# Experts of middle rank as 64- and 32-place float32 units instead of three-pass float32r, in one layer of a hybrid network on Trainium2

## The chip, the cores and the metric

One core of one Trainium2 chip. The metric is device time in microseconds (us) of one execution. The kernel before was timed three times: 1410.18, 1393.49 and 1408.15 us, median 1408.15.

## What is computed

One layer: RMSNorm, an input projection, four parallel sequence branches, an output projection with residual, then a mixture of experts with its own RMSNorm, router and residual, and a final RMSNorm. There are 512 tokens of width 1024, all float32. The change touches the mixture of experts alone:

```python
logits = xt @ router_w + router_b
top_logits, top_idx = lax.top_k(logits, 4)
gates = softmax(top_logits)
# for each of 32 experts e, for the tokens that chose it:
hmid = xt[tok] @ w_gu[e] + b_gu[e]                # 1024 -> 2048
glu  = minimum(hmid[:, 0::2], 7.0)
lin  = clip(hmid[:, 1::2], -7.0, 7.0)
act  = glu * sigmoid(1.702 * glu) * (lin + 1.0)
y    = act @ w_down[e] + b_down[e]                # 1024 -> 1024
out[tok] += gate * y
```

Each expert has 8 MB of `w_gu` and 4 MB of `w_down`, so 384 MB of weights pass through the core once.

## The kernel before

The first 350 us compute the branches and the router. Then `moe` (L495) runs the 32 experts one after the other in an order written as a string, `SEQ` (L56). The experts are ranked on the chip by how many tokens chose them; a rank has a fixed number of places (`HCAP`, `LCAP`, L53), and tokens beyond it go to an extra loop that runs only if there are any.

An expert is one or two *units* (class `Unit`, L513):

- **H** (heavy; ranks 0 to 12, up to 128 places): the tokens' activations stand still in TensorE, the weights stream past as float32r. For the precision of float32 weights and activations are each split in a high and a low part, and three products are made: high by high, high by low, low by high (`three`, L640). Weights are split by `Splits.make` (L619): ScalarE writes the high part (L627), VectorE the low part (L628), for 1024 columns at a time, into one of `NSP` = 3 buffers `w2`. A heavy expert needs 24 such splits.
- **L** (light; 64 places): plain float32 matmuls straight from the weights (L672, L741). The 2048 hidden columns are two output halves that stand on partitions 0 to 63 and 64 to 127, so two matmuls run side by side.
- **B** (32 places): the same with four matmuls side by side. Only rank 0 has one, for its places 129 to 160, beside its H unit; this pair is called the big expert below.

The loop at L866 works on expert j: the first product `gemm1` over eight 1 MB weight chunks k (L887), the activation function `act` (L677), then the second product `gemm2` of expert j-1 over eight halves f of its down chunks (L930), so that the activation of j is hidden behind it. `back` (L693) transposes the activated values of j for its own `gemm2`. `yout` (L746) multiplies by the gate and makes high and low parts of the result on ScalarE and VectorE; for a unit of 32 places that is four instructions on each, for one of 64 two. `hot` makes a 0/1 matrix S of places and tokens, and `add` (L784) scatters the results of all pending units with a matmul (S by result) into the accumulator of 128 tokens, which VectorE adds (L803). Additions are made whenever the expert before was heavy: one of the four in front of each of the first four steps f of its `gemm2`, or, after the big expert, four in a row.

The tokens of the units come by `prepare` (L818: 0/1 matrix, token numbers by four matmuls `ids`, gathering DMA) and `turn` (L586: eight transposes, then copies from two PSUM banks). `where` (L808 to L815) says at which point of which expert a group is turned: A is inside `gemm1`, M is between `act` and `gemm2`, B is in `gemm2`. The weight chunks go through 11 buffers, in order, by DMAs of SyncE (`Loads`, L189): a chunk's buffer is free when its last reader is done, which for a heavy expert is VectorE's split and for the others TensorE. PSUM: `bank()` has two buffers in `moe`, shared by the results of `gemm2`, `ids` and `turn`; `pair()` has two of two banks; `hL` one.

Of the kernel before, what the change touches and what calls it, by code (L numbers as in the profile page):

```python
# [47 lines left out]
NE = 32  # L48
# [3 lines left out]

HCAP, BASE, LCAP = (128, 120, 104, 104, 96, 96, 88, 80, 80, 72, 72, 72, 72), 32, 64  # L53
NHV = len(HCAP)

SEQ, BIG = "LL" + 4 * "HLHLL" + 5 * "HL", 2  # L56
NSP = 3
FIN = "aaqqrAQrASQrAQrSSS"


def moe_consts(tc, a, keep, ra, early, ident, gcol, bgu, bd):
# [45 lines left out]
    cap = c["cap"] = keep.tile([96, NE], F32, name="cap")  # L107
    nc.gpsimd.memset(cap, float(LCAP))
    for r, n in enumerate(HCAP):
        nc.gpsimd.memset(cap[:, r:r + 1], float(n + (BASE if r == 0 else 0)))  # L110

# [102 lines left out]
class Router:  # L214
# [132 lines left out]
    def places0(r):  # L347

        nc = r.nc
        x0 = r.wk.tile([128, 1024], F32, tag="yL", name="x0")  # L350
        xp = r.wk.tile([128, KD, 128], F32, name="xp")
# [143 lines left out]
def moe(ctx, tc, a, out, acc, c, loads, rt, mp, mp_es, hp, s2p, bp, early):  # L495
# [29 lines left out]

    H, L = list(range(1, NHV)), list(range(NHV, NE))
    seq, nh = [], 0
    for x in SEQ:
        if x == "H":
            r = 0 if nh == BIG else H.pop(0)  # L530
            nh += 1
            seq.append([Unit("H", r, HCAP[r])] + ([Unit("B", 0, BASE, HCAP[0])] if r == 0 else []))
        else:
            seq.append([Unit("L", L.pop(0) if len(seq) > 1 else L.pop(-1), LCAP)])
    N = len(seq)
# [5 lines left out]

    groups, rest = [], []
    for j, us in enumerate(seq):
        for u in us:
            u.j = j
            if j < 2:
                continue
            if u.kind == "H":
                groups.append([(u, 0)])
            else:  # L550
                if len(rest) % 2 == 0:
                    groups.append([])
                    open_ = groups[-1]
                open_.append((u, 64 * (len(rest) % 2)))
                rest.append(u)
    tg = wk.tile([128, Unit.made + 1, 2], F32, name="tg")
# [29 lines left out]
    def turn(g, rows, m, banks):  # L586
# [5 lines left out]
        else:  # L592
            xp = wk.tile([128, KD, 128], F32, name="xp")
            for u_, o in groups[g]:
# [65 lines left out]
    def gemm1(us, chunk, k, splits, limit):  # L660
# [3 lines left out]
        for u in us:  # L664
# [79 lines left out]
    ny = [0]  # L744

    def yout(us):  # L746

        for u in us[::-1]:
            if u.kind == "H":
                n = u.n  # L750
                u.yH = wk.tile([128, 2, 512], FR, name="yH")[0:n]
                u.yL = wk.tile([128, 2, 512], FR, name="yL")[0:n]
                for j in range(2):
# [3 lines left out]
                continue  # L757
            ny[0] += 1
            u.yS = (bp if ny[0] % 2 else wk).tile([128, 2, 512], FR, tag="yS", name="yS")
            y = u.y[0]  # L760
# [48 lines left out]
    for g, us in enumerate(groups):  # L809
        j = us[0][0].j  # L810
        where.setdefault((("M" if len(seq[j - 1]) > 1 else "A"), j - 1) if seq[j - 1][0].kind == "H" else ("B", j - 1) if j > 1 and seq[j - 2][0].kind == "H" else
                         ("M", j - 1), []).append(g)
    for (x, j), gs in list(where.items()):
        if x == "B" and len(gs) > 1:
            where[("M", j)] = where.get(("M", j), []) + [gs.pop(0)]  # L815
    have, hots, turned = {}, set(), set()
# [22 lines left out]
    two = lambda: [bank(), bank()]  # L839
    halves2 = lambda: (lambda h: [h[:, 0:512], h[:, 512:1024]])(pair())  # L840

    def steps(*gens):
# [23 lines left out]
    for j, us in enumerate(seq):  # L866
# [9 lines left out]
        if j == 0:  # L876
            u.views, u.h = [(0, rt.h0[0])], rt.h0[1]
        else:
            light = lambda: [pair() if j < 2 else hL.tile([128, 1024], F32, name="hL")]
            for x in us:  # L880
                if x.kind == "H":
                    x.bk = [pair(), pair()]
                bias(x, x.bk if x.kind == "H" else light() if x.kind == "L" else [light()[0][:, 0:512]])
        hi = heavy.index(j) if kind == "H" else 0
        after = heavy.index(j - 1) if j and seq[j - 1][0].kind == "H" else None
        for k in range(KD):
# [18 lines left out]
            if kind == "L" and j > 1:  # L905
                if k == 3:
# [8 lines left out]
        prev = seq[j - 1]  # L915
        pk = prev[0].kind
        if pk == "H":
            hot(pending)
            limit = (after, 24) if kind != "H" and not (j + 1 < N and seq[j + 1][0].kind == "H") else (after + 1, 16)
            if len(prev) > 1:  # L920
                for i in range(NT):
                    add(pending, i)
        else:
            limit = None
        if j == 1:
            bd = rt.bdown()
        for f in range(KD):
            if pk == "H" and len(prev) == 1 and pending and f < NT:
                add(pending, f)
            gemm2(prev, loads.of(j - 1), f, splits, limit)  # L930
            if j == 1:
                run(bd, 1)
            elif pk == "L" and f in (2, 5):
                prepare()
            if pk == "H" and f == 4 and kind == "L":
                back(us)
            if pk == "H" and f == 5:
                turn_at("B", j, halves2)
            if pk == "L" and j + 1 < N and seq[j + 1][0].kind == "H" and f > 4:
                splits.make((heavy.index(j + 1), 16), 1)  # L940
        if pk == "H":
            pending = []
        pending = pending + prev
        yout(prev)
        if not (pk == "H" and kind == "L"):
            back(us)
# [1075 lines left out]
```

## Time and profile before

| | us |
|---|---|
| median of three runs | 1408.15 |
| lowest, highest | 1393.49, 1410.18 |
| the profiled execution | 1399.37 |
| its span, first to last instruction | 1397.5 |
| TensorE busy in it | 1326.4 |
| VectorE, ScalarE busy | 898.3, 633.0 |

The rows further down are of this one execution. In lists of busy time an engine's name stands with its time and count of instructions. PE is TensorE's matmuls, PEld its weight loads, DVE VectorE, ACT ScalarE, POOL GpSimd, SPq the queue of SyncE that issues DMAs. "128*64" in a matmul row means 128 contracted rows by 64 stationary columns. A float32 matmul has two records in the trace, so four matmuls are eight records.

### The profile page before, as it was taken

The numbers are of one execution on the slowest core, as the hardware profiler recorded it, in microseconds if no ns is written. First come the engines' busy times: TensorE is split into PE (matmuls) and PEld (weight loads), VectorE is DVE, ScalarE is ACT, GpSimd is POOL, SyncE is SP. The second block draws the span as 40 slices with busy tenths as digits, with TensorE's granted clock in tenths as the row PEclk, the third lists the DMA queues.
The fourth block names the chain that finished last, engine by engine and source line by source line (L and its number), as shares of the span: only waits on it lengthen the run. The fifth ranks groups of instructions, "written<-read, shape, count | busy, mean of one in ns | idle before, by whom it ended". The sixth has DMA issues, their size and how long they took to land.

```text
span 1397.5 us, 17808 instructions
## 1 busy us (share of the span) xinstructions
PE 1326.4 (95%) x6462; PEld 780.8 (56%) x6462; DVE 898.3 (64%) x1204; ACT 633.0 (45%) x872; POOL 144.4 (10%) x196
## 2 busy tenths in 40 slices
PE   7999998898999999898999999999999999999995
PEld 6878773674365554455545645546534646464552
DVE  5457867796486754557546764758535768585855
ACT  5467665641254533335324542526324546362632
POOL 0000126352100001000010000200010000000001
PEclk9999997998999999999999999999999999999997
DMA  6322021156999999987999999999999999999961
GB/s 204 103 64 87 1 106 50 53 201 259 407 401 404 420 418 400 367 345 287 407 375 419 420 392 420 409 419 405 420 398 419 419 387 414 417 395 404 389 269 77
DMA packets 80657, 442.09 MB, mean 316 GB/s; under 512 B 10956, under 2 KB 25364, under 8 KB 31540
## 3 DMA queue, kind: packets, MB, share of 16 engines
q1 hardware_dynamic: 76564, 427.66, 76.7%
q0 software_dynamic: 3856, 12.72, 2.7%
q8 instruction: 52, 0.85, 0.2%
q10 hardware_dynamic: 144, 0.52, 0.1%
q14 instruction: 41, 0.34, 0.1%
HBM read 436.68 MB, written 4.19 MB: 315 GB/s over the span
## 4 chain that ended last, share of the span: by engine, by line
PE 82%; DVE 8%; ACT 5%; issue 2%; POOL 1%; DMA 1%; DVEq 0%; POOLq 0%; ACTq 0%
PE h L643 20%; PE hL L672 17%; PE m L643 10%; PE m L741 10%; PE h L801 6%; PE m L1191 6%; PE h L672 2%; PE h L708 1%; PE m L1195 1%; PE h L658 1%; DVE wos L1815 1%; PE m L1820 1%; DMA rows<-xdr,ix 1%; PE hL L658 1%; PE h L1820 1%
## 5 line engine op out<-in xcount | busy, mean ns | idle before, releaser
L628 DVE TENSOR_TENSOR w<-wch,w 128x1024 fp32r<-128x1024 f32 x312 | 379.1, 1224 | 124.4 <-ACT w L627 116.3
L627 ACT ACTIVATE w<-wch 128x1024 fp32r<-128x1024 f32 x312 | 329.2, 1062 | 244.4 <-PE m L643 109.3
L643 PE MATMUL h<-w,xx 128*72 128x512 f32 (+6 forms) x1248 | 300.1, 398 | 0.6 <-DVE w L628 0.6
L643 PEld LDWEIGHTS h<-w,xx 128*72 128x72 f32 (+6 forms) x1248 | 195.5, 158 | 96.9 <-issue 6.3
L672 PE MATMUL hL<-wch,xp 128*64 128x512 f32 (+1 forms) x1152 | 245.5, 593 | 0.0
L672 PEld LDWEIGHTS hL<-wch,xp 128*64 128x64 f32 (+1 forms) x1152 | 78.4, 135 | 150.6 <-issue 146.9
L741 PE MATMUL m<-wch,aTL 128*64 128x512 f32 x608 | 140.9, 609 | 11.3 <-DVE xx L611 7.4
L687 ACT ACTIVATE ag<-ag 128x512 f32<-128x512 f32 (+7 forms) x46 | 28.8, 627 | 200.2 <-DVE ag L686 200.1
L643 PE MATMUL m<-w,aH 128*72 128x512 f32 (+6 forms) x416 | 114.8, 398 | 0.0
L579 POOL CAST ix<-tg 64x1 int32<-64x1 f32 (+8 forms) x31 | 18.4, 594 | 854.6 <-DVE tg L571 846.6
L741 PEld LDWEIGHTS m<-wch,aTL 128*64 128x64 f32 x608 | 41.6, 139 | 91.5 <-issue 76.8
L643 PEld LDWEIGHTS m<-w,aH 128*72 128x72 f32 (+6 forms) x416 | 64.1, 158 | 27.3 <-issue 1.7
L803 DVE TENSOR_TENSOR acc<-acc,h 128x1024 f32<-128x1024 f32 (+1 forms) x61 | 72.9, 1198 | 6.8 <-PE h L801 6.8
L775 DVE SCALAR_TENSOR_TENSOR yS<-m,tg,yS 64x512 fp32r<-64x512 f32 x36 | 27.0, 750 | 75.4 <-ACT yS L773 75.1
L773 ACT ACTIVATE yS<-m,tg 64x512 fp32r<-64x512 f32 x36 | 24.6, 682 | 107.3 <-PE m L741 107.0
L686 DVE TENSOR_SCALAR ag<-hL 128x512 f32<-128x512 f32 (+1 forms) x18 | 12.2, 676 | 94.6 <-PE hL L672 94.6
L1191 PE MATMUL m<-uH,wh 128*128 128x512 f32 x176 | 71.9, 408 | 0.8 <-DVE uL L1298 0.8
L1191 PE MATMUL m<-uH,wl 128*128 128x512 f32 x176 | 70.1, 398 | 0.3 <-DVE wl L1157 0.3
L1191 PE MATMUL m<-uL,wh 128*128 128x512 f32 x176 | 69.7, 396 | 0.0
L643 PE MATMUL m<-w,aL 128*72 128x512 f32 (+6 forms) x208 | 65.1, 394 | 0.0
L801 PE MATMUL h<-yS,S 128*128 128x512 f32 (+1 forms) x168 | 56.2, 417 | 2.1 <-DVE acc L803 1.0
L1157 DVE TENSOR_TENSOR wl<-wnat,wh 128x1024 fp32r<-128x1024 f32 (+1 forms) x26 | 31.5, 1223 | 30.3 <-ACT wh L1156 30.3
(488 smaller groups left out, 1695.4 us busy)
## 6 DMA issues: line engine op xcount, KB each, us to landing
wch<-in_moe_w_gu_dram SPq DMA_DIRECT2D x256, 1024.0 KB
wch<-in_moe_w_down_dram SPq DMA_DIRECT2D x127, 1024.0 KB
wnat<-in_w_in_dram SPq DMA_DIRECT2D x12, 1024.0 KB
wch<-in_w_out_dram SPq DMA_DIRECT2D x4, 1024.0 KB
xin<-in_x_dram SPq DMA_DIRECT2D x4, 512.0 KB
acc<-in_x_dram SPq DMA_DIRECT2D x4, 512.0 KB
xdr<-wch POOLq DMA_DIRECT2D x4, 512.0 KB, 8.0
out_dram<-fo SPq DMA_DIRECT2D x4, 512.0 KB
```

Source lines behind the costliest of these rows:

```text
L627: nc.scalar.activation(wh, w, AF.Copy)
L628: nc.vector.tensor_tensor(wl, w, wh.bitcast(F32), op=OP.subtract)
L643: nc.tensor.matmul(ps_[q], x, w[:, 512 * q:512 * q + 512], start=start and z == 0, stop=stop and z == 2)
L658: nc.tensor.matmul(u.h[q], u.sel.to_broadcast([96, n]), c["bgu"][:, 512 * q:512 * q + 512], start=True, stop=False)
L672: nc.tensor.matmul(u.h[q], u.xT[:, k, :], W[:, 512 * q:512 * q + 512], start=False, stop=last)
L687: nc.scalar.activation(g, g, AF.Gelu_apprx_sigmoid)
L741: nc.tensor.matmul(u.y[0][64 * dh:64 * dh + 64, :], u.aT[:, 2 * (f // 4) + f % 2, (f // 2) % 2, :], W[:, 512 * dh:512 * dh + 512], start=f ...
L801: nc.tensor.matmul(hh[:, 512 * dh:512 * dh + 512], s, y, start=z == 0, stop=z == len(todo) - 1)
L803: nc.vector.tensor_tensor(o, o, hh[:, cols], op=OP.add)
L1157: nc.vector.tensor_tensor(wl, w, wh.bitcast(F32), op=OP.subtract)
L1191: nc.tensor.matmul(s.p, s.ws[q // 2][:, k, :], u_[:, k, :], start=(k == 0 and q == 0), stop=(k == KD - 1 and q == 2))
L1820: nc.tensor.matmul(p, m_(x, k)[:, 128 * i:128 * i + 128], ww, start=(k == 0 and q == 0), stop=(k == KD - 1 and q == 2))
```

## The change

Ranks 1, 2, 3 and the first 128 places of rank 0 stay H. Ranks 4 to 12 become pairs of an L and a B unit (64 + 32 = 96 places; `X` in the new string). Ranks 13 to 28, and 30 and 31, stay L. Rank 29 becomes a B unit alone (32 places). In a pair the B unit takes its weight chunks two at a time, after every second chunk of the L unit. The buffers of splits go from three to two; token tiles `xp` from one to two, S from three to four, and results rotate through four tiles. After a pair, as after the big expert, the four additions stand in a row before `gemm2`. Light experts and pairs are transposed back at f = 5 always, groups are turned inside `gemm1` wherever the expert isn't the big one, and the second product's PSUM of a pair's B unit is a `bank()`.

```diff
-HCAP, BASE, LCAP = (128, 120, 104, 104, 96, 96, 88, 80, 80, 72, 72, 72, 72), 32, 64
-SEQ, BIG = "LL" + 4 * "HLHLL" + 5 * "HL", 2
-NSP = 3
+CAPS = (160, 120, 104, 104) + 9 * (96,) + 16 * (64,) + (32, 64, 64)
+SEQ, BIG = "LL" + "HLHLL" + 2 * "HLXLL" + "XLXLL" + "XLXLXLXBXL", 2
+NSP = 2
...
+        elif x == "X":
+            r = cols[x].pop(0)
+            seq.append([Unit("L", r, 64), Unit("B", r, 32, 64)])
...
-                for q in range(4):
-                    nc.tensor.matmul(u.h[q], u.xT[:, k, :], W[:, 512 * q:512 * q + 512], start=False, stop=last)
+                two_ = u.kind == "B" and us[0].kind == "L"
+                for k_ in ((k - 1, k) if two_ and k % 2 else () if two_ else (k,)):
+                    W = chunk(k_)
+                    for q in range(4):
+                        nc.tensor.matmul(u.h[q], u.xT[:, k_, :], W[:, 512 * q:512 * q + 512], start=False, stop=k_ == KD - 1)
...
-                u.y = [pair()[:, 0:512]] if u.kind == "B" else [bank()[0:u.m, :] for _ in range(2 if u.kind == "H" else 1)]
+                u.y = [pair()[:, 0:512]] if u.kind == "B" and us[0].kind == "H" else [bank()[0:u.m, :] for _ in range(2 if u.kind == "H" else 1)]
...
+    def ytile():
+        ny[0] += 1
+        return ((wk, "yH"), (wk, "yL"), (wk, "yS"), (bp, "yS"))[ny[0] % 4]
...
-                u.S = wk.tile([128, T], FR, name="S", bufs=3)[0:u.m]
+                u.S = wk.tile([128, T], FR, name="S", bufs=4)[0:u.m]
...
+        j = us[0][0].j - 1
+        where.setdefault(("M" if j < 2 or seq[j][0].kind == "H" and len(seq[j]) > 1 else "A", j), []).append(g)
...
-            if kind == "H" and k == 2:
+            if k == (2 if kind == "H" else 5):
                 turn_at("A", j, two)
...
+        zone = pending and (pk == "H" or len(prev) > 1)
+        if zone:
             hot(pending)
             if len(prev) > 1:
                 for i in range(NT):
                     add(pending, i)
...
-            if pk == "H" and f == 4 and kind == "L":
+            if f == 5 and kind != "H":
                 back(us)
```

The order on TensorE near the end of the program, before: the last heavy expert's last step of `gemm1` (`w,xx`), the light expert before it in `gemm2` (`wch,aTL`), the last light expert's `gemm1` (`wch,xp`), and the first of four additions (`yH`, `yL`, `yS` by `S`) with the heavy `gemm2` (`w,aH` and `w,aL`) behind it.

```order
L643 MATMUL h<-w_9708,xx 72x512 x6
L741 MATMUL m<-wch,aTL 64x512 x16
L708 MATMUL h<-ident,av 128x72 x8
...
L672 MATMUL hL<-wch,xp 64x512 x32
L801 MATMUL h<-yH,S 128x512
L801 MATMUL h<-yL,S 128x512
L801 MATMUL h<-yS,S 128x512
...
L643 MATMUL m<-w_9818,aH 72x512 x4
L643 MATMUL m<-w_9818,aL 72x512 x2
```

The same place now, from the last chunks of the last pair's `gemm1`: `aT` and `avB` are those of B units.

```order
L681 MATMUL hL<-wch,xp 64x512 x8
L681 MATMUL h<-wch,xp 32x512 x8
L745 MATMUL m<-wch,aT 32x512 x12
L717 MATMUL hL<-ident,av 128x128 x4
L708 MATMUL h<-ident,avB 128x128 x2
...
L681 MATMUL hL<-wch,xp 64x512 x32
L816 MATMUL h<-yS,S 128x512 x24
L750 MATMUL m<-wch,aTL 64x512 x4
L745 MATMUL m<-wch,aT 32x512 x4
```

Matmuls of 64 and of 32 columns alternate now in both products of a pair, and the 24 matmuls of the four additions stand in front of all of `gemm2`.

VectorE at the very end of the program, before: the last heavy expert's low parts `yL`, the S matrices, then the additions.

```order
L756 SCALAR_TENSOR_TENSOR yL<-m,tg,yH 72x512 x2
L782 TENSOR_SCALAR S<-iota,tg 72x512
L782 TENSOR_SCALAR S<-iota,tg 128x512
L803 TENSOR_TENSOR acc<-acc,h 128x1024 x4
L764 SCALAR_TENSOR_TENSOR yS<-m,tg,yS 128x512
```

And now, with a pair in that place:

```order
L790 SCALAR_TENSOR_TENSOR yS<-m,tg,yS 32x512 x4
L790 SCALAR_TENSOR_TENSOR yS<-m,tg,yS 64x512 x2
L797 TENSOR_SCALAR S<-iota,tg 128x512 x3
L818 TENSOR_TENSOR acc<-acc,h 128x1024 x4
L779 SCALAR_TENSOR_TENSOR yS<-m,tg,yS 128x512
```

Six instructions and three S matrices stand where there were two and two.

## Rows read from the trace of the kernel before

**Rows 1.** The page: busy time by engine, and the chain that ended last

```profile
PE 1326.4 (95%) x6462; PEld 780.8 (56%) x6462; DVE 898.3 (64%) x1204; ACT 633.0 (45%) x872; POOL 144.4 (10%) x196
PE 82%; DVE 8%; ACT 5%; issue 2%; POOL 1%; DMA 1%; DVEq 0%; POOLq 0%; ACTq 0%
```

**Rows 2.** Busy time by stretch; last three columns: granted clock, DMA share, GB/s

```profile
660.00:1320.00 660.00, 653.70 (x3077) 352.97 (x3077) 425.74 (x481) 294.72 (x342) 28.11 (x31) 0.99 1.01 408
...
633.00:639.90 6.90, 4.23 (x11) 2.78 (x11) 3.98 (x6) 1.46 (x3) 0.00 (x0) 0.51 0.48 202
...
875.00:900.00 25.00, 24.53 (x116) 13.44 (x117) 17.19 (x19) 13.99 (x16) 5.56 (x2) 0.93 1.01 405
...
1350.00:1375.00 25.00, 23.61 (x101) 13.14 (x101) 16.33 (x16) 6.70 (x8) 0.00 (x0) 1.00 0.02 7
```

**Rows 3.** The chain that ended last, 1262 to 1335 us: start, us, what

```profile
1269.25 13.74 PE hL L672 x64
1282.99 1.59 PE h L801 x6
1284.58 1.38 PE m L643 x6
1285.96 1.41 PE h L801 x6
...
1301.80 22.33 PE h L643 x96
1324.13 7.02 PE m L741 x32
```

**Rows 4.** TensorE in time, 540 to 640 us; in brackets idle before, and releaser

```profile
544.28 0.40 PE L658 MATMUL hL<-bgu,PMb 96*32 96x512 bf16 x4 [0.56 <-ACT aTL L720]
...
547.60 1.07 PE L672 MATMUL hL<-wch,xp 128*32 128x512 f32 x8
548.60 3.07 PE L643 MATMUL h<-w,xx 128*128 128x512 f32 x12
551.60 1.07 PE L672 MATMUL hL<-wch,xp 128*32 128x512 f32 x8
...
583.32 0.24 PE L570 MATMUL m<-mv,G 128*128 128x6 bf16 x4 [0.25 <-DVE tg L571]
...
635.67 1.01 PE L658 MATMUL h<-bgu,PMb 96*104 96x512 bf16 x2 [5.38 <-DVE yS L775]
```

**Rows 5.** Waits summed: engine, line, releaser, us, times, longest

```profile
PE m L741 <- DVE xx L611: 7.4, 4, 1.9
```

**Rows 6.** ScalarE in time, 898 to 904 us

```profile
901.14 1.07 ACT L627 ACTIVATE w<-wch 128x1024 fp32r<-128x1024 f32 x1 [0.32 <-PE h L643]
902.51 1.07 ACT L627 ACTIVATE w<-wch 128x1024 fp32r<-128x1024 f32 x1 [0.31 <-PE h L643]
```

**Rows 7.** VectorE in time, 898 to 904 us

```profile
902.24 1.23 DVE L628 TENSOR_TENSOR w<-wch,w 128x1024 fp32r<-128x1024 f32 x1 [0.16 <-ACT w L627]
```

**Rows 8.** VectorE in time, 1346 to 1368 us

```profile
1346.60 0.69 DVE L686 TENSOR_SCALAR ag<-hL 128x512 f32<-128x512 f32 x1 [7.44 <-PE hL L672]
...
1348.61 1.21 DVE L803 TENSOR_TENSOR acc<-acc,h 128x1024 f32<-128x1024 f32 x1
```

**Rows 9.** ScalarE in time, 627 to 637 us

```profile
629.80 2.75 ACT L773 ACTIVATE yS<-h,tg 32x512 fp32r<-32x512 f32 x4
```

**Rows 10.** VectorE in time, 627 to 637 us

```profile
632.59 3.03 DVE L775 SCALAR_TENSOR_TENSOR yS<-h,tg,yS 32x512 fp32r<-32x512 f32 x4 [1.50 <-ACT yS L773]
```

**Rows 11.** TensorE in time, 1355 to 1398 us

```profile
1365.31 1.08 PE L741 MATMUL m<-wch,aTL 128*64 128x512 f32 x4 [1.32 <-DVE yL L756]
```

**Rows 12.** Groups by shape from 400 us on: count, busy us, mean ns, idle before

```profile
L628 DVE TENSOR_TENSOR w<-wch,w 128x1024 fp32r<-128x1024 f32 x305 | 370.7, 1224 | 121.8 <-ACT w L627 114.1 <-DMA wch<-in_moe_w_down_dram 0.2
L627 ACT ACTIVATE w<-wch 128x1024 fp32r<-128x1024 f32 x304 | 320.9, 1062 | 241.2 <-PE m L643 109.3 <-PE h L643 67.9 <-DMA wch<-in_moe_w_down_dram 59.9
L643 PE MATMUL h<-w,xx 128*72 128x512 f32 x384 | 91.8, 397 | 0.0
```

More of the change, by code (lines that the diff above doesn't have):

```diff
@@ L107, in moe_consts @@
     cap = c["cap"] = keep.tile([96, NE], F32, name="cap")
-    nc.gpsimd.memset(cap, float(LCAP))
-    for r, n in enumerate(HCAP):
-        nc.gpsimd.memset(cap[:, r:r + 1], float(n + (BASE if r == 0 else 0)))
+    for n in sorted(set(CAPS), reverse=True):
+        r = CAPS.index(n)
+        nc.gpsimd.memset(cap[:, r:] if n == 64 else cap[:, r:r + CAPS.count(n)], float(n))
     mv = c["mv"] = keep.tile([128, NT, NTB, 6], BF, name="mv")
@@ L350, in places0 @@
         x0 = r.wk.tile([128, 1024], F32, tag="yL", name="x0")
-        xp = r.wk.tile([128, KD, 128], F32, name="xp")
+        xp = r.wk.tile([128, KD, 128], F32, name="xp", bufs=2)
         for b in range(2):
@@ L524, in __init__ @@
                 u.pos, u.mv, u.sel = posP[:, :, col:col + 1], mv[:, :, col, :], PMb[:, col:col + 1]
-    H, L = list(range(1, NHV)), list(range(NHV, NE))
+    cols = {x: [r for r, n in enumerate(CAPS) if n in ns] for x, ns in
+            (("H", range(97, 129)), ("X", (96,)), ("L", (64,)), ("B", (32,)))}
     seq, nh = [], 0
@@ L529, in moe @@
         if x == "H":
[L530 removed]
+            r = 0 if nh == BIG else cols[x].pop(0)
             nh += 1
[L532 removed]
+            seq.append([Unit("H", r, min(CAPS[r], 128))] + ([Unit("B", 0, 32, 128)] if r == 0 else []))
+        elif x == "X":
+            r = cols[x].pop(0)
+            seq.append([Unit("L", r, 64), Unit("B", r, 32, 64)])
         else:
[L534 removed]
+            seq.append([Unit(x, cols[x].pop(0 if len(seq) > 1 else -1), 64 if x == "L" else 32)])
     N = len(seq)
@@ L539, in moe @@
         seq[e][0].sel = rt.sel0[:, e:e + 1]
-    groups, rest = [], []
+    groups, at = [], 128
     for j, us in enumerate(seq):
@@ L549, in moe @@
                 groups.append([(u, 0)])
[L550 to L555, printed above, removed]
+                continue
+            at = -(-at // u.n) * u.n
+            if at + u.n > 128:
+                groups.append([])
+                open_, at = groups[-1], 0
+            open_.append((u, at))
+            at += u.n
     tg = wk.tile([128, Unit.made + 1, 2], F32, name="tg")
@@ L592, in turn @@
         else:
-            xp = wk.tile([128, KD, 128], F32, name="xp")
+            xp = wk.tile([128, KD, 128], F32, name="xp", bufs=2)
             for u_, o in groups[g]:
@@ L744, in moe @@
     ny = [0]
+    def ytile():
+        ny[0] += 1
+        return ((wk, "yH"), (wk, "yL"), (wk, "yS"), (bp, "yS"))[ny[0] % 4]
     def yout(us):
         for u in us[::-1]:
+            new = []
+            for _ in range(2 if u.kind == "H" else 1):
+                pool, tag = ytile()
+                new.append(pool.tile([128, 2, 512], FR, tag=tag, name="yS"))
             if u.kind == "H":
                 n = u.n
-                u.yH = wk.tile([128, 2, 512], FR, name="yH")[0:n]
-                u.yL = wk.tile([128, 2, 512], FR, name="yL")[0:n]
+                u.yH, u.yL = (x[0:n] for x in new)
                 for j in range(2):
@@ L757, in yout @@
                 continue
-            ny[0] += 1
-            u.yS = (bp if ny[0] % 2 else wk).tile([128, 2, 512], FR, tag="yS", name="yS")
+            u.yS = new[0]
             y = u.y[0]
@@ L809, in moe @@
     for g, us in enumerate(groups):
[L810 to L815, printed above, removed]
+        j = us[0][0].j - 1
+        where.setdefault(("M" if j < 2 or seq[j][0].kind == "H" and len(seq[j]) > 1 else "A", j), []).append(g)
     have, hots, turned = {}, set(), set()
@@ L878, in moe @@
         else:
-            light = lambda: [pair() if j < 2 else hL.tile([128, 1024], F32, name="hL")]
+            light = lambda: pair() if j < 2 else hL.tile([128, 1024], F32, name="hL")
             for x in us:
@@ L882, in moe @@
                     x.bk = [pair(), pair()]
-                bias(x, x.bk if x.kind == "H" else light() if x.kind == "L" else [light()[0][:, 0:512]])
+                bias(x, x.bk if x.kind == "H" else [light()] if x.kind == "L" else [(pair() if us[0].kind == "L" else light())[:, 0:512]])
         hi = heavy.index(j) if kind == "H" else 0
@@ L902, in moe @@
                 prepare()
-            if kind == "H" and k == 2:
+            if k == (2 if kind == "H" else 5):
                 turn_at("A", j, two)
-            if kind == "L" and j > 1:
+            if j > 1 and kind != "H":
                 if k == 3:
@@ L916, in moe @@
         pk = prev[0].kind
+        soon = j + 1 < N and seq[j + 1][0].kind == "H"
+        zone = pending and (pk == "H" or len(prev) > 1)
+        limit = None
         if pk == "H":
+            limit = (after, 24) if kind != "H" and not soon else (after + 1, 16)
+        if zone:
             hot(pending)
-            limit = (after, 24) if kind != "H" and not (j + 1 < N and seq[j + 1][0].kind == "H") else (after + 1, 16)
             if len(prev) > 1:
@@ L927, in moe @@
         for f in range(KD):
-            if pk == "H" and len(prev) == 1 and pending and f < NT:
-                add(pending, f)
+            if zone and len(prev) == 1:
+                if f < NT:
+                    add(pending, f)
             gemm2(prev, loads.of(j - 1), f, splits, limit)
@@ L932, in moe @@
                 run(bd, 1)
-            elif pk == "L" and f in (2, 5):
+            elif len(prev) == 1 and pk != "H" and f in (2, 5):
                 prepare()
-            if pk == "H" and f == 4 and kind == "L":
+            if f == 5 and kind != "H":
                 back(us)
-            if pk == "H" and f == 5:
-                turn_at("B", j, halves2)
-            if pk == "L" and j + 1 < N and seq[j + 1][0].kind == "H" and f > 4:
+            if pk != "H" and soon and f > 4:
                 splits.make((heavy.index(j + 1), 16), 1)
-        if pk == "H":
+        if zone:
             pending = []
@@ L944, in moe @@
         yout(prev)
-        if not (pk == "H" and kind == "L"):
+        if kind == "H":
             back(us)
```

4 lines of the change are left out of this document (removed).

## The prediction

> **What bounds the kernel now.** I read the page first: TensorE is busy for 95% of the span, and the chain that ended last runs over it for 82% [rows 1]. Then the stretches, for a mean hides who limits the experts. From 660 to 1320 us TensorE is busy 653.70 of 660 us, and in the same stretch the DMA share is 1.01 at 408 GB/s [rows 2]: both are full. Which of them sets the end is seen where they part. In 1350 to 1375 the DMA share is 0.02 while TensorE is busy for 23.61 of 25 us [rows 2], so the last weights land some 45 us before the end. ScalarE waited for weights for 59.9 us in all, since it splits ahead [rows 12], but TensorE's chain goes to a DMA for only 1% of the span [rows 1]. So TensorE is the bound, with the transfers close behind: VectorE and ScalarE (425.74 and 294.72 of the 660 us) have room. The change takes much from the two that have room. What counts is what it does to TensorE's time and to its waits.
>
> **The pairs in place of nine heavy experts.** Taken away on the other engines: 9 x 24 = 216 splits of 1.06 us on ScalarE and 1.22 us on VectorE [rows 12], 229 and 264 us of busy time. I cost this at nothing, because the cover is TensorE: it did not wait for splits (0.0 us idle before the 72-column matmuls [rows 12]).
>
> On TensorE a heavy expert takes 22.33 us for the first product and 8 x 1.39 = 11.1 us for the second, 33.4 in all [rows 3]. An L unit takes 13.74 + 7.02 us for 64 and 32 records, 0.215 us a record [rows 3]. The one B unit that there is shows the price of 32 columns: eight records start at 547.60, the heavy matmuls behind them at 548.60, and the next eight at 551.60 [rows 4]. At four side by side, half of 0.215, eight records would be 0.86 us, and twelve heavy matmuls are 22.33 / 8 = 2.79 us; the round took 4.00, so 0.35 us goes for going to 32 columns and back. A pair alternates four times in each product: 13.74 + 64 x 0.107 + 4 x 0.35 = 22.0 us, and 7.02 + 32 x 0.107 + 4 x 0.35 = 11.8 us. Together 33.8, against 33.4. So nine pairs cost **+4 us**; the additions have as many matmuls as before (two for yH and yL, now one for each unit). That 64 to 32 columns costs what 128 to 32 does is not shown. From below I take no price for the alternation, 31.0 us a pair, -21 us in nine; from above the price of the big expert for every single chunk, 8 x 0.35 in the first product, 35.2 us, +16. I keep to +4, since the row is of the same matmuls.
>
> The Trainium skill, in "TensorEngine Tiling (Array Packing)", Key Properties, says that changing the tiling mode, not just the tile, drains TensorE. By this the pair pays at each alternation, which is the 0.35 us that the big expert shows; by the page's table of theoretical speedups alone, up to 4x for 32 columns, the sum would be the lower bound of 31.0. The trace stands with the drain.
>
> **Rank 29 with 32 places** replaces 20.8 us by (64 + 32) x 0.107 and two entries at some 0.2, 10.6: **-10 us**.
>
> **Two buffers of splits** for the four experts that stay heavy. A buffer's round now: ScalarE starts the high part at 901.14, the low part on VectorE ends at 902.24 + 1.23 = 903.47 [rows 6, 7], 2.33 us. TensorE then uses the buffer for 22.33 / 16 = 1.40 us, and its last matmul is done about 0.2 us after the next one's start, for a record lasts 0.40 and they start 0.23 apart [rows 3, 12]. That is 3.9 us, three buffers give one split in 1.31, under TensorE's 1.40. With two it would be 1.96; but the first two of the six matmuls need the high part alone, 0.47 us that lie beside VectorE, so (3.9 - 0.47) / 2 = 1.73, 0.33 more than now. Queued behind the waiting matmul are all of TensorE's own. In the first product 14 splits stall (two are made ahead), in the second those behind the additions, about four: 18 x 0.33 = 6 us for an expert. The big expert has 1.2 us of its B unit behind every second split, which covers it. Three experts: **+18 us**. Bounds: 0, if pauses elsewhere hide it, and 3 x 20 x 0.56 = 34, if the high part gives no overlap.
>
> **Waits that go.** After the big expert TensorE idled 5.38 us for a PSUM pair [rows 4] and then had the lower clock, 1.2 of 2.4 GHz: the mean of 0.51 of 633.00 to 639.90 [rows 2], 4.2 us of it busy, half of which is lost. Now the B unit's bias takes the other pair: -7.5. Four groups turned between `act` and `gemm2` stopped TensorE for 7.4 us [rows 5], and after two of these the clock was down as well (0.93 of a 25 us stretch, one of two alike [rows 2]: 1.75 us each); they are turned inside `gemm1` now, with chunks left to cover the copies: -11. One wait of 0.56 for the transposed values [rows 4] goes: -0.5. Together **-19 us**. Nothing gives a loss here; the gain is nil if `turn` only waits elsewhere, so 0 to -19.
>
> **Waits that come.** Four additions in a row need a PSUM pair each, of two. VectorE comes to the first one 2.0 us after `gemm1` ended (1346.60 to 1348.61 [rows 8]) and takes 1.21 for each; with six matmuls an addition takes TensorE 1.41 [rows 3]. The third would start at 2.8 and gets its pair at 3.3: 0.5 us at some six zones, **+3**. Nine more units need token numbers, four matmuls of 0.24 together [rows 4]: **+2**. At the end the last expert's `gemm2` waits for its bank until `yout` of the expert before is done, 1.32 us now [rows 11]. Of a pair, the B unit alone takes 2.75 on ScalarE and then 3.03 on VectorE [rows 9, 10], the L unit two more there at 0.76, so 7.3 us, and VectorE makes the S matrices only behind that. Behind the waiting matmul stand all of the last additions. **+7** with a little of the lower clock; bounds +3 (other bank first) and +10. The weight queue has 228 more gathered rows of 4 KB, 0.9 MB, 2 us at 408 GB/s, covered as long as TensorE is the later one.
>
> **The sum** is 4 - 10 + 18 - 19 + 3 + 2 + 7 = +5, of terms whose errors are larger, with more bounds below than above. Against the profiled execution, 1399.4 us, that would be 1404. That execution lies 9 us under the median of 1408.15. I take 1402: no change.
>
> **Rivals.** *Faster:* the alternation is free and the pauses absorb the missing buffer: -21 - 10 - 19 + 12 = -38 by TensorE. The transfers allow less: from 660 us on they have no pause to give [rows 2], and TensorE can only eat up its distance behind them, about 20 us, besides the 10 that it gains before 660. About 1370 us. For it speaks that going from 64 to 32 columns is a smaller step than from 128; against it, the 0.35 us in every round of the one example.
>
> The Trainium skill, "HBM Reference", Specifications (TRN2), gives about 425 GB/s for a core that streams alone; this trace has 408 over 660 us, so by the page too the transfers would have at most 4% to give there.
>
> *Transfers bind already:* what TensorE gains behind 660 us is waited away, and only its losses count: two split-starved experts before 660 (+12), the big expert's wait (-7.5), the tail (+7). 1411 us. The last transfer would then land at the same time as now and TensorE would wait for `wch`; against it, no such wait of TensorE's in the chain [rows 1].
>
> *Slower:* the two-buffer round is not overlapped (34 for 18), pairs pay for each chunk (16 for 4), and the groups' copies stop TensorE at their new place (-8 for -19). The first decides: from 1.96 us a split on, heavy experts are bound by VectorE, and its other work adds to each. 1399 + 5 + 16 + 12 + 11 = 1443 us; with the first alone 1420. For it: VectorE's 1.23 with idle 0.16 between two splits [rows 7] leaves it little room.
>
> *The places don't fit:* a token too many would start the extra loop, a heavy expert of 33.4 us with nothing beside it, over 40 us. With these inputs the reference's router gives counts of 130, 115, 100, 97, then 92 to 69 in ranks 4 to 12, and 32 in rank 29: they fit, the last exactly. 2 in 100.
>
> **How the numbers follow.** Forecast 0.50, faster 0.20, transfers 0.12, slower 0.16, places 0.02. A measurement here tells about 2%, 28 us, from no change, so 1380 and 1436 are the limits. Faster than 1380: most of the faster rival and little else, 0.16. Slower than 1436: half of the slower rival, the places, little else, 0.11. Same 0.73. The range of 1370 to 1432 leaves out the far end of the slower rival and a part of the faster one.
>
> **What would show it.** Right: heavy `gemm1` of some 27 us where 22.3 stood, with TensorE waiting for VectorE's split; pairs at 22 and 12 us; no waits for `xx` copies or of 5 us behind the big expert; a wait of 7 us ahead of the last `gemm2`; DMA share still 1.0 from 660 on. Wrong: heavy experts at 22 us, pairs at 31 or below, or TensorE waiting for weight chunks.

## The result, and the profile after

The changed kernel takes 1423.95 us (median of four runs, 1421.13 to 1425.57), the kernel before 1404.34 (four runs, 1393.49 to 1410.18): a ratio of 1.0159, 95% interval 1.0118 to 1.0199. I had forecast no change, 1402. The time lies in the range of 1370 to 1432, the direction is wrong: it is slower, by 20 us where I had a sum of +5. The four runs of the kernel before were few: beside the experiments, 10 to 17 runs of it on a chip have medians of 1398.70 to 1399.46, and against these the loss is 25 to 26 us.

The profiled execution took 1421.13 us. Its page, where it answers to [rows 1] and [rows 12]:

```profile
span 1419.4 us, 18082 instructions
...
PE 1327.0 (93%) x6946; PEld 651.9 (46%) x6946; DVE 666.4 (47%) x1026; ACT 430.4 (30%) x685; POOL 127.0 (9%) x197
...
L633 DVE TENSOR_TENSOR w<-wch,w 128x1024 fp32r<-128x1024 f32 x96 | 116.8, 1225 | 62.2 <-ACT w L632 59.9
L632 ACT ACTIVATE w<-wch 128x1024 fp32r<-128x1024 f32 x96 | 100.9, 1058 | 77.3 <-PE h L648 35.8
L648 PE MATMUL h<-w,xx 128*104 128x512 f32 (+2 forms) x384 | 98.7, 404 | 14.8 <-DVE w L633 13.4
```

VectorE gave up 232 us of work and ScalarE 203, as the change means to, and TensorE's busy time is what it was. So the 21.9 us by which the span grew are idle time of TensorE and matmuls that start later than they could. The view of waits names the engine that waits, then the releaser; its numbers are the sum, the count and the longest in us:

```profile
PE h L648 <- DVE w L633: 13.4, 23, 0.9
...
PE hL L663 <- ACT aTL L729: 7.5, 10, 0.8
PE m L750 <- issue: 6.0, 1, 6.0
PE h L816 <- DVE acc L818: 3.0, 7, 0.5
```

The first, third (the wait at the end) and fourth line are terms of my sum. The second is not: ten waits of a bias matmul (L663) for ScalarE's copy of aTL (L729).

Where the time went shows best from expert to expert. The kernels have the same order of experts (a pair stands where a later heavy expert stood), so I took the start of each expert's first bias matmul from TensorE's timeline and subtracted. An interval holds the expert's first product and the second product and additions of the one before it.

| intervals (experts counted from 0) | before | after | change |
| --- | --- | --- | --- |
| up to expert 2 | 388.56 | 387.26 | -1.3 |
| heavy 2, 4, 12, each with the light one behind | 193.69 | 218.05 | +24.4 |
| the big expert 7 and 8 | 86.96 | 88.52 | +1.6 |
| 9, with the wait behind the big expert | 38.89 | 31.55 | -7.3 |
| second light ones 6, 11, 16, 21 | 105.58 | 96.53 | -9.1 |
| other pairs and light ones up to 27 | 422.49 | 439.34 | +16.9 |
| 28 to 30, around rank 29 | 96.00 | 85.29 | -10.7 |
| 31 to the end of the span | 65.35 | 72.88 | +7.5 |

The transfers do not look like the reason. The share that was 1.01 at 408 GB/s [rows 2] is 0.99 at 398 now, and 0.88 in a stretch where a heavy expert waits for splits; the view of waits has none of TensorE's for a weight chunk. The control below tests it (columns: TensorE, its weight loads, VectorE, ScalarE, GpSimd busy, granted clock, DMA share, GB/s):

```profile
475.00:500.00 25.00, 23.32 (x106) 11.48 (x108) 15.38 (x19) 10.03 (x13) 0.00 (x0) 1.00 0.88 333
...
660.00:1320.00 660.00, 641.38 (x3424) 245.59 (x3422) 213.55 (x312) 111.12 (x169) 17.67 (x39) 1.00 0.99 398
```

### The profile page after: what moved, and what is told of

Same layout as the page of the kernel before. It is cut to its first block, busy times and chain, and to the rows that moved or that the text cites. A ratio compares the mean times of both kernels' runs of the same rounds, so it can differ in the third digit from the quotient of the medians.

```text
span 1419.4 us, 18082 instructions
## 1 busy us (share of the span) xinstructions
PE 1327.0 (93%) x6946; PEld 651.9 (46%) x6946; DVE 666.4 (47%) x1026; ACT 430.4 (30%) x685; POOL 127.0 (9%) x197
## 5 line engine op out<-in xcount | busy, mean ns | idle before, releaser
L681 PE MATMUL hL<-wch,xp 128*64 128x512 f32 (+1 forms) x1728 | 373.0, 596 | 0.0
L681 PEld LDWEIGHTS hL<-wch,xp 128*64 128x64 f32 (+1 forms) x1728 | 117.7, 134 | 220.1 <-issue 211.8
L750 PE MATMUL m<-wch,aTL 128*64 128x512 f32 x864 | 204.6, 607 | 9.8 <-issue 6.0
L790 DVE SCALAR_TENSOR_TENSOR yS<-m,tg,yS 64x512 fp32r<-64x512 f32 (+1 forms) x92 | 68.9, 749 | 227.2 <-ACT yS L788 226.0
L633 DVE TENSOR_TENSOR w<-wch,w 128x1024 fp32r<-128x1024 f32 x96 | 116.8, 1225 | 62.2 <-ACT w L632 59.9
L632 ACT ACTIVATE w<-wch 128x1024 fp32r<-128x1024 f32 x96 | 100.9, 1058 | 77.3 <-PE h L648 35.8
L648 PE MATMUL h<-w,xx 128*104 128x512 f32 (+2 forms) x384 | 98.7, 404 | 14.8 <-DVE w L633 13.4
L750 PEld LDWEIGHTS m<-wch,aTL 128*64 128x64 f32 x864 | 55.7, 137 | 122.0 <-issue 108.9
L681 PE MATMUL h<-wch,xp 128*32 128x512 f32 (+1 forms) x704 | 100.9, 604 | 0.2 <-ACT xp L365 0.2
L816 PE MATMUL h<-yS,S 128*128 128x512 f32 (+2 forms) x376 | 95.7, 410 | 4.2 <-DVE acc L818 3.0
L816 PEld LDWEIGHTS h<-yS,S 128*128 128x128 f32 (+2 forms) x376 | 68.1, 192 | 29.8 <-DVE acc L818 7.1
L729 ACT ACTIVATE aTL<-hL 128x512 f32<-128x512 f32 x25 | 14.9, 596 | 215.6 <-PE m L750 212.9
L788 ACT ACTIVATE yS<-m,tg 64x512 fp32r<-64x512 f32 (+1 forms) x92 | 62.6, 680 | 31.4 <-PE m L750 24.6
```

The source lines that it names most:

```text
L632: nc.scalar.activation(wh, w, AF.Copy)
L633: nc.vector.tensor_tensor(wl, w, wh.bitcast(F32), op=OP.subtract)
L648: nc.tensor.matmul(ps_[q], x, w[:, 512 * q:512 * q + 512], start=start and z == 0, stop=stop and z == 2)
L681: nc.tensor.matmul(u.h[q], u.xT[:, k_, :], W[:, 512 * q:512 * q + 512], start=False, stop=k_ == KD - 1)
L750: nc.tensor.matmul(u.y[0][64 * dh:64 * dh + 64, :], u.aT[:, 2 * (f // 4) + f % 2, (f // 2) % 2, :], W[:, 512 * dh:512 * dh + 512], start=f ...
L788: nc.scalar.activation(u.yS[s_, dh, :], y[s_, :], AF.Copy, scale=u.gate[s_, :])
```

## The experiments

Theory A in the expectations: TensorE sets the time, and the lost time is in stalls of its own that can be given back one by one. Theory B: the transfers set it, and what TensorE gains comes back as waits for chunks. Each ratio is to runs of the kernel before on the same chip.

### The changed kernel again

> The changed kernel as it is, beside the other three on one chip: about 1424 us, 1.016 of before; it leaves out nothing and adds nothing, and is there for the differences to the other runs.

1424.74 us, ratio 1.0182 (1.0150 to 1.0215): 26 us over the kernel before on this chip. The differences below are taken from this and the next run.

### Three split buffers, and the control for the room they take

```diff
-RING, MORE, THIRD = 8, 2, 1
+RING, MORE, THIRD = 8, 2, 0
```

(and the pool of the third kind of chunk buffer goes; the second run has `NSP = 3` as well)

> The changed kernel with one chunk buffer fewer (10 instead of 11), still two buffers of splits: the control of the next run. Theory A (TensorE sets the time, its lost 22 us are stalls of its own): no change, 1424 us within 5, since the weight queue has idle spells (DMA share 0.88 in 475 to 500 us, 0.68 in 625 to 650) and the last chunk lands some 50 us before the end. Theory B (the transfers set the pace behind 660 us, where the DMA share is 0.99): a chunk of look-ahead less is paid for in waits for chunks, 1430 us or more.

> As the run before (10 chunk buffers), with three buffers of splits instead of two; the one edit between the two is the number of split buffers. Theory A: the three experts that stall for splits lose 5.7 to 8.0 us each in their own interval and 1.6 us in the next, 24.4 together by the intervals from bias to bias, and get back nearly all: 24 us faster than the control, about 1400, heavy first products back at 22.5 us. My prediction's term was 18: about 1406. Theory B: what two of them gain before 660 us is kept (15 us), the rest is waited away for chunks: about 1409. If pauses elsewhere had hidden the missing buffer: no change.

The control: 1424.5 us. A chunk buffer less costs nothing, against theory B. With three split buffers: 1406.03 us, ratio 1.0046 (1.0031 to 1.0061), 18.5 us faster. That is my term of +18, and 6 less than the intervals had promised. The round, first with two buffers, on ScalarE, VectorE and TensorE (start, duration, operation, in brackets the idle time before it and what ended it):

```profile
745.04 1.06 ACT L632 ACTIVATE w<-wch 128x1024 fp32r<-128x1024 f32 x1 [1.13 <-PE h L648]
746.43 1.06 ACT L632 ACTIVATE w<-wch 128x1024 fp32r<-128x1024 f32 x1 [0.33 <-PE h L648]
748.63 1.06 ACT L632 ACTIVATE w<-wch 128x1024 fp32r<-128x1024 f32 x1 [1.14 <-PE h L648]
```

```profile
746.13 1.23 DVE L633 TENSOR_TENSOR w<-wch,w 128x1024 fp32r<-128x1024 f32 x1 [0.97 <-ACT w L632]
747.52 1.23 DVE L633 TENSOR_TENSOR w<-wch,w 128x1024 fp32r<-128x1024 f32 x1 [0.16 <-ACT w L632]
```

```profile
747.42 3.04 PE L648 MATMUL h<-w,xx 128*104 128x512 f32 x12 [0.55 <-DVE w L633]
```

A buffer comes round after 748.63 - 745.04 = 3.59 us, two splits in that time, 1.80 for one. I had 2.33 + 1.40 + 0.2 - 0.47 = 3.46, so 1.73. Each engine waits in turn for the other two, and none is full. With three buffers TensorE of the same expert runs 21 matmuls without a pause:

```profile
734.70 4.99 PE L648 MATMUL h<-w,xx 128*104 128x512 f32 x21
```

### Two buffers for aTL

```diff
-                u.aT = wk.tile([128, 4, 2, 64], F32, name="aTL")
+                u.aT = wk.tile([128, 4, 2, 64], F32, name="aTL", bufs=2)
```

> The changed kernel with two buffers for the transposed values of a light unit (aTL) instead of one. Theory A: the ten waits of 0.75 us of the bias matmuls before a light expert that follows a pair or a light expert come from ScalarE's copy, which starts only when the second product of the expert before has read the one buffer out (1226.26 end of the last matmul, 1226.37 start of the copy, the transposes done since 1224.16). With two they go: 7.5 us faster, about 1416, in the trace no wait over 0.3 us before that bias. Rival (the transposes come too late, since back stands at the sixth of eight steps): the waits stay, no change. Theory B: the waits go and come back as waits for chunks, no change.

1409.23 us, ratio 1.0078 (1.0058 to 1.0098): 15.3 us faster than the control on the same chip, twice what the waits add up to. TensorE and ScalarE at such a place in the changed kernel:

```profile
1223.41 0.75 PE L717 MATMUL hL<-ident,av 128*128 128x128 f32 x4
...
1224.33 1.94 PE L750 MATMUL m<-wch,aTL 128*64 128x512 f32 x8
1227.02 0.62 PE L663 MATMUL hL<-bgu,PMb 96*64 96x512 bf16 x4 [0.76 <-ACT aTL L729]
```

```profile
1226.37 0.60 ACT L729 ACTIVATE aTL<-hL 128x512 f32<-128x512 f32 x1 [7.13 <-PE m L750]
```

The transposes (L717) are done at 1224.16, ScalarE has been idle for 7.13 us, and yet the copy starts only when the last L750 has read the old aTL, at 1226.27. The next expert's bias needs hL, which that copy empties. The same place with two buffers:

```profile
1212.99 0.60 ACT L729 ACTIVATE aTL<-hL 128x512 f32<-128x512 f32 x1 [4.90 <-PE hL L717]
```

```profile
1213.06 1.94 PE L750 MATMUL m<-wch,aTL 128*64 128x512 f32 x8
1214.83 0.60 PE L663 MATMUL hL<-bgu,PMb 96*64 96x512 bf16 x4
```

Now the transposes release the copy, and the bias does not wait. Nine of the ten intervals are 0.83 to 0.95 us shorter where 0.76 was idle (33.09 to 32.14, 31.55 to 30.62), 8.2 together. The tenth, 24, is 2.4 shorter; some 1.5 of that is a lower clock that this trace does not have there (last section). The rest I had not foreseen. Where a heavy expert follows, the copy that waits holds up ScalarE's queue, and the splits stand behind it. In the changed kernel:

```profile
733.46 0.60 ACT L729 ACTIVATE aTL<-hL 128x512 f32<-128x512 f32 x1 [6.70 <-PE m L750]
733.96 2.00 ACT L632 ACTIVATE w<-wch 128x1024 fp32r<-128x1024 f32 x2
```

Heavy experts 2 and 12 went from 39.90 and 39.12 to 37.99 and 37.22, 3.8 together. That makes 13 without the clock and 14.5 with it; the profiled span is 13.1 shorter than that of the changed kernel, mainly since the part before expert 2 took 1.1 longer.

### The end

```diff
-                u.y = [pair()[:, 0:512]] if u.kind == "B" and us[0].kind == "H" else
+                u.y = [hL.tile([128, 1024], F32, name="hL")[:, 0:512]] if u.halves else [pair()[:, 0:512]] if u.kind == "B" and us[0].kind == "H" else
...
         gemm2(seq[-1], loads.of(N - 1), f, splits, None)
-        if f < NT:
-            add(pending, f)
+    for i in range(NT):
+        add(pending, i)
```

> The changed kernel with another end: the last expert's second product goes to the PSUM tile that its first product has left, instead of a bank that the pair's output still holds, and the four additions of the units before stand behind it instead of between its steps. Theory A: the wait of 5.99 us before the last second product goes, and so does the 0.79 before the last additions, with some 1.7 us of the lower clock (granted 0.86 in 1375 to 1400): 7 us faster, about 1417, unless TensorE then waits for the pair's S matrices and scaled outputs, which VectorE makes some 7 us after the pair's second product: the last expert's own 7.0 us of matmuls just cover that. Rival (VectorE and ScalarE bound the end): 2 us faster at most.

1416.48 us, ratio 1.0115 (1.0095 to 1.0134), 8 us faster. Before the edit, then after it:

```profile
1385.43 1.98 PE L750 MATMUL m<-wch,aTL 128*64 128x512 f32 x4 [5.99 <-issue]
```

```profile
1383.12 7.09 PE L750 MATMUL hL<-wch,aTL 128*64 128x512 f32 x32
1391.26 2.19 PE L816 MATMUL h<-yS,S 128*128 128x512 f32 x8 [1.05 <-DVE S L797]
```

The product covers VectorE's work on the pair's output all but 1.05 us. The term of +7 was right.

### Two units in a group

```diff
-            if at + u.n > 128:
+            if at + u.n > 128 or len(groups[-1]) == 2:
```

> The changed kernel with at most two units in a gathered group (one group of three there is: the pair of the 29th expert in order and rank 29). Theory A: the wait of 2.28 us at 1150.24 comes from that group: three one-hot tables want three of two G buffers, the third stands in VectorE's queue until TensorE has read the first, and behind it wait the S matrices and the copy of xp that TensorE's bank waits for. With two per group the wait goes, and the 1.7 us lost to the lower clock behind it: 4 us faster, about 1420. Rival (VectorE is late there for another reason, the two S matrices): the wait stays, no change.

1420.21 us, ratio 1.0158 (1.0133 to 1.0183): 4.5 us by the medians, which the interval cannot tell from nothing. The place can. VectorE in the changed kernel, then TensorE:

```profile
1148.00 0.69 DVE L568 TENSOR_TENSOR G<-posP,iota 128x512 bf16<-128x512 f32 x1 [15.12 <-PE m L575]
1148.61 0.88 DVE L797 TENSOR_SCALAR S<-iota,tg 128x512 fp32r<-128x512 f32 x2
1149.49 0.69 DVE L610 COPY xp<-m 128x512 f32<-128x512 f32 x1
```

```profile
1150.24 0.36 PE L575 MATMUL m<-mv,G 128*128 128x6 bf16 x8 [2.29 <-DVE xp L610]
```

VectorE stood for 15.12 us before the third G table, whose buffer TensorE's own later matmul (L575) frees; the xp copy stood behind it, and TensorE waits for that. With two in a group the copy starts when the transposes are done, and interval 24 is 33.08 us for 37.12.:

```profile
1145.54 0.69 DVE L610 COPY xp<-m 128x512 f32<-128x512 f32 x1 [8.71 <-PE m L604]
```

Not all of these 4 us are the wait. In two runs that keep the wait without the lower clock behind it (two aTL and fours, last section), the interval comes to some 35.6 us with their own savings added back, so about 2.5 are the wait and 1.5 the clock.

### The 32-place units in fours

```diff
-                for k_ in ((k - 1, k) if two_ and k % 2 else () if two_ else (k,)):
+                for k_ in (range(k - 3, k + 1) if two_ and k % 4 == 3 else () if two_ else (k,)):
```

(and in the second product of a pair the same, two chunks for one)

> The changed kernel with the 32-place unit of a pair run for four chunks in a row instead of two, in both products: half as many changes between 64 and 32 columns. My prediction's price, 0.35 us for going there and back: 2 x 0.35 in each product of nine pairs, 12.6 us faster. By the trace of the changed kernel a round of the first product takes 5.44 us, 0.29 over the time of its 32 records, one of the second 2.86, 0.25 over it: 2 x 0.29 + 2 x 0.25, nine times, 9.7 us faster, about 1414. Rival (the alternation is free, as the table of speedups alone would have it): no change. Theory B: chunks are held longer, TensorE waits for chunks, slower than 1424.

1415.24 us, ratio 1.0127 (1.0108 to 1.0147), 9.5 us faster, and 36 goings there and back fewer: 0.26 us each. By the intervals it is a little less: against the changed kernel's second trace those from 9 on, without 24 and its clock, are 7.9 us shorter for 34 of them, 0.23 each. In the changed kernel the rounds of the second product are seen in the starts:

```profile
1250.96 1.06 PE L745 MATMUL m<-wch,aT 128*32 128x512 f32 x8
1251.96 1.94 PE L750 MATMUL m<-wch,aTL 128*64 128x512 f32 x8
1253.82 1.07 PE L745 MATMUL m<-wch,aT 128*32 128x512 f32 x8
```

1253.82 - 1250.96 = 2.86 for a round; 8 x 0.215 + 8 x 0.107 = 2.58 would be free of a price. The rival of a free alternation falls, and 0.35, the price from the big expert, was a little high for the step from 64 to 32 columns.

### Rank 29 with 64 places

```diff
-CAPS = (160, 120, 104, 104) + 9 * (96,) + 16 * (64,) + (32, 64, 64)
+CAPS = (160, 120, 104, 104) + 9 * (96,) + 16 * (64,) + (64, 64, 64)
```

> The changed kernel with rank 29 at 64 places again, as a light unit in the same place of the order. By the prediction's term 10 us slower than the changed kernel; by the intervals from bias to bias (9 to 11 us less around it than in the kernel before) 10.8 less one more wait of 0.95 for aTL: 1434 to 1436. Theory B (transfers): no change, since its weights are as many bytes with either.

1431.95 us, ratio 1.0234 (1.0199 to 1.0268), 7.2 us slower, where 10 to 12 were expected. The intervals 28 to 30 grow by 12.8 (85.29 to 98.09), but 24 falls from 37.12 to 33.08: without the 32-place unit there is no group of three. So the term of -10 was right at its place, and rank 29 gave 4 us of it back at another.

### All edits, with pairs and with thirteen heavy experts

> The changed kernel with all edits so far: three split buffers with 10 chunk buffers, two aTL, two units in a group, the 32-place units in fours, the other end. Theory A (the gains add): 18 + 13 + 4 + 10 + 8 off 1424, 1371 us. Theory B (with the stalls gone the transfers bind, DMA share 1.00 at 406 GB/s behind 660 us already with two aTL alone): the last chunk lands not before 1350 and the end comes 35 us behind it at least, 1385 us.

> As the run with all edits (1381.0 us), but the 32-place units for two chunks in a row again, as in the changed kernel. Theory A (TensorE alone): the 9 us that the fours gave come back, 1390. Theory B (with all edits in, the transfers bind behind 660 us; TensorE waited 4.6 us for chunks there, and units in fours hold chunks longer): about the same, 1381 to 1384, with fewer waits for chunks.

1381.02 us, ratio 0.9874 (0.9855 to 0.9893), and 1380.91, ratio 0.9870 (0.9838 to 0.9903): both beat both kernels. Theory A's 1371 is missed by 10, and the fours, worth 9.5 us alone, add nothing here. TensorE's waits in the run with fours, and some of them in time:

```profile
PE hL L681 <- DMA wch<-in_moe_w_gu_dram: 4.6, 10, 0.7
```

```profile
1322.26 1.94 PE L681 MATMUL hL<-wch,xp 128*64 128x512 f32 x8 [0.55 <-DMA wch<-in_moe_w_gu_dram]
1324.75 1.94 PE L681 MATMUL hL<-wch,xp 128*64 128x512 f32 x8 [0.56 <-DMA wch<-in_moe_w_gu_dram]
1327.24 1.94 PE L681 MATMUL hL<-wch,xp 128*64 128x512 f32 x8 [0.55 <-DMA wch<-in_moe_w_gu_dram]
```

They stand above all in intervals 23 and 31, which are 2.2 and 2.4 us longer than in the run without the fours, while most intervals around pairs are 0.4 to 0.6 shorter: most of what the fours gain is waited away. Without the fours there is no such line, and the weights are as full as TensorE:

```profile
660.00:1320.00 660.00, 656.66 (x3562) 248.99 (x3560) 221.46 (x325) 117.08 (x176) 18.70 (x39) 1.00 1.01 412
```

So theory B, wrong of the changed kernel, comes true of the fours some 40 us below it. Of the other four edits it is not shown: alone they gave 18.5, 15.3, 4.5 and 8.0 us, 46 together, and the run that has these four is 44 us faster than the changed kernel on the same chip. The other side, with the changed kernel's code, three split and ten chunk buffers, first without the edits at aTL, groups and end, then with them:

```diff
-CAPS = (160, 120, 104, 104) + 9 * (96,) + 16 * (64,) + (32, 64, 64)
+CAPS = (160, 120, 104, 104, 96, 96, 88, 80, 80, 72, 72, 72, 72) + 16 * (64,) + (32, 64, 64)
...
-SEQ, BIG = "LL" + "HLHLL" + 2 * "HLXLL" + "XLXLL" + "XLXLXLXBXL", 2
+SEQ, BIG = "LL" + 4 * "HLHLL" + "HLHLHLHBHL", 2
```

> The changed kernel's code with the thirteen heavy experts of the kernel before in place of the pairs, three buffers of splits and 10 chunk buffers: all of the change but the pairs (rank 29 with 32 places, turn and back at their new places, four y buffers). Theory A: against the kernel before, rank 29 gives 10.8, the wait behind the big expert 7.5, the stalls of two light experts in a row 9, less 3 for waits of aTL: 24 us faster than before, about 1376. Theory B: in the kernel before the transfers were as full (DMA share 1.01 behind 660 us) as TensorE, so what is gained behind 660 us is waited away for chunks, and what stays is the gain of before 660 and some of TensorE's distance behind the weights: 8 to 14 us, 1386 to 1392. Then the waits are ScalarE's for wch and TensorE's for w.

> The thirteen heavy experts (1393.7 us before this edit) with two aTL, two units in a group and the other end. Theory A: three heavy experts behind two light ones began with late splits, since ScalarE stood before its aTL copy until TensorE had read the one buffer (889.19, the splits right behind it; the interval is 35.05 us for 32.35 in the kernel before, 33.61 for 31.48 and 33.81 for 31.09), 2 to 3 us each, and the wait of 1.32 before the last second product goes: 9 us faster, 1385. Theory B: the transfers are full behind 660 us (1.01 at 408 GB/s) and the last chunk landed at 1357 of 1395: what TensorE gains is waited away, 1390 to 1394. If theory A holds, the pairs (1381.0 with all edits) are worth no more than 4 us; if B, some 10.

1393.7 us, ratio 0.9964 (0.9949 to 0.9979), then 1386.04, ratio 0.9907 (0.9874 to 0.9940). The first is slower than both theories had it (1376, and 1386 to 1392); 7.5 us of theory A's gain was to be the wait behind the big expert, which did not go. The second step is theory A's (9 us faster expected, 7.7 found); the copy of aTL had held up the splits here too:

```profile
889.19 0.60 ACT L729 ACTIVATE aTL<-hL 128x512 f32<-128x512 f32 x1 [6.48 <-PE m L750]
889.68 2.94 ACT L632 ACTIVATE w<-wch 128x1024 fp32r<-128x1024 f32 x3
```

With the same edits in both, pairs are 5 us faster than heavy experts (1380.91 against 1386.04, on one chip). More than that is at one place: interval 9 takes 30.62 us with pairs and 39.28 with heavy experts, since the wait behind the big expert stays with a heavy neighbour, [rows 4] once more. In the rest from expert 2 on, the pairs are 4.4 us slower in the two traces. The wait:

```profile
PE h L663 <- DVE yS L790: 5.4, 1, 5.4
```

## Why the prediction was wrong

The step that failed is in "Waits that go": "One wait of 0.56 for the transposed values [rows 4] goes: -0.5", and then "Nothing gives a loss here". I read the wait of the one place where the trace of before had it, and took the new place of `back` as the cure. I did not ask which buffer the moved copy writes. `back` now runs in the second product of a light expert or a pair as well, aTL has one buffer which that product reads to its end, and with pairs for heavy experts light units now follow each other on the one hL through most of the order, so that a bias waits for the copy. So a term of -0.5 is one of +13 to +15 us (the run with two aTL). With two aTL the kernel is 10 us slower than the kernel before (1409.23 against 1399.46), with one it is 25 (the control, 1424.5, on the same chip); my sum without this term is +5.5.

The 1402 leaned on a second thing: I made 1404 of the profiled execution, 1399.4, and the sum, set it against the median of three runs, 1408.15, and called it no change. By the later medians of 1399 the profiled execution was the typical one, and the sum stood for 5 us slower.

The other terms, against the runs:

- *Two split buffers, +18:* 18.5. The round was 0.07 us a split too short. Of the 24.4 in the intervals three buffers give back 17.5 (summed over the six intervals, against the control), and 3.8 belong to aTL; the other 3 I did not trace. Nothing hid the missing buffer.
- *Pairs, +4:* the products were right. In intervals 26 and 27, L681, L750 and L745 take 54.5 us without the wait, the heavy and light matmuls of before 54.7; my 33.8 and 20.8 make 54.6. What I did not price is around them: transposes of a 128-place group 1.02 us for 0.47, biases 1.31 for 1.13, each summed from start to start in the two traces. That is some 0.7 us a pair, 6 to 7 in all.
- *Three units in a group, not in the sum:* +4, some 2.5 of it from a VectorE queue that waits for TensorE, the rest the clock behind that. I had counted the group's gathered rows and not its G tables, which are what has two buffers.
- *Waits that go, -19:* -16.4 (7.3 behind the big expert, 9.1 at the second light ones). Three waits for aTL are counted in these intervals; with two aTL they are 2.8 us shorter, so that the term without the failed step comes to -19. That the B unit's bias is what saves the 7.3 is shown by the thirteen heavy experts, where the wait is back.
- *Rank 29, -10:* -10.7 by the intervals (12.8 by the run with 64 places), and its group of three takes 4 of that, as above.
- *Row additions, +3, and the end, +7:* 2.2, five of the seven waits in the line of L816 (the other two stand at the end, as in the kernel before), and 8.
- *Token numbers, +2:* 1.5 in the intervals of the table's sixth row (L575 takes 2.7 us from start to start, L570 before 1.2).
- *Transfers bind already:* wrong of this kernel, as argued; the control with ten chunks costs nothing, and the single edits gave what TensorE's own stalls had promised. In the repaired kernel it is right of the fours alone.

The other errors are small beside the one term with the wrong sign: without it 10 us stand against +5.5, and the group of three is most of the difference. My "more bounds below than above" was the same mistake: I had allowed no loss for an edit that moves a copy ahead of the last reader of its buffer.

The Trainium skill, "TensorEngine Tiling (Array Packing)", Key Properties, says that a change of tiling mode drains TensorE. The run in fours agrees that the change costs time: 0.23 to 0.26 us for going to 32 columns and back.

## What to carry to other kernels

When a copy is moved earlier, look up the last reader of the buffer that it writes, not only what it reads: with one buffer the move gains nothing, and what is queued behind the copy is late with it. Where work changes its kind, count the buffers of every tile that the new kind takes, for each place in the order where two of them now follow each other. An edit that frees an engine which nobody waits for leaves the time to what the edit costs elsewhere: of 435 us freed on two engines, nothing showed. With four small stalls mended the pairs are 5 us ahead of heavy experts, and that is a wait of TensorE's that they happen to avoid.

## What I had not expected of the hardware

The lower clock did not follow from the wait alone. The wait of 2.29 us before L575 is in the changed kernel and in the run with two aTL, and the four microseconds behind it were at a granted clock of 0.57 in one and 1.00 in the other (columns as above):

```profile
1150.00:1154.00 4.00, 3.61 (x16) 1.27 (x18) 3.46 (x11) 1.05 (x2) 1.54 (x4) 0.57 1.00 409
```

```profile
1141.40:1145.40 4.00, 3.80 (x24) 1.47 (x26) 3.35 (x10) 1.05 (x2) 1.54 (x4) 1.00 0.97 397
```

Seven traces have this wait; five show the lower clock behind it, those with two aTL and in fours do not. Nor does the code decide it: both traces of the changed kernel, the one above and the run again, have a wait of 2.56 us before L750 behind the big expert, and the eight microseconds after it were at 1.00 in the first (592.10 to 600.10) and at 0.79 in the second (592.50 to 600.50). Interval 7 is 48.94 us in the one and 50.63 in the other.

What decides between the two is open. So the 1.7 us that such a stretch costs should not be counted as part of an edit that removes one wait. The start of expert 2 also differs by 8 us between the two runs with all edits (391.73 and 383.50 in their TensorE timelines), though nothing differs in their code up to there; 5.8 of it is there before the first expert (326.44 and 320.62). This, too, stays unexplained; it is a reason to compare two traces interval by interval and not by their spans.
